# Attention of a hybrid residual block: TensorE in the written order, and 128 columns in place of padded 256

## The chip, the cores and the metric

The kernel runs on one core of a Trainium2 chip. The metric is the device time of one execution in microseconds (us). The engines are TensorE (PE, with its weight loads shown apart as PEld), VectorE (DVE), ScalarE (ACT), GpSimd (POOL) and SyncE (SP), which issues most of the transfers. Matrix products are written to PSUM, which has eight banks of 128 partitions x 512 fp32.

## The reference

One layer over x of shape (1, 512, 1024), all in fp32:

```
xn = rmsnorm(x)
q, k, v, xr, gr, ga, gb = split(xn @ W_in)          # each 512 x 1024
ya = chunked_band_attention(q, k, v, rel_table) @ W_attn_out
yb = (rg_lru(conv(xr)) * gelu(gr)) @ W_rnn_out
h  = x + (sigmoid(ga) * ya + sigmoid(gb) * yb) @ W_o
h  = h + (silu(g) * up) @ W_ffn_out                 # g, up = split(rmsnorm(h) @ W_ffn_in)
out = rmsnorm(h)
```

The attention has 16 heads of width 64. A frame belongs to a chunk of 64 and reads its own chunk and the eight before it, so over 512 frames it reads all earlier chunks: the probabilities are block lower triangular. A learned bias on the clipped distance is added to the scores, and a softmax follows.

## The kernel before

Precision: each fp32 operand is split into a high and a low part of type float32r (`split`, L78: ACT copies the high part, DVE subtracts to get the low one), and a product is three matmuls, high x high, high x low and low x high (`mm3`, L72, lines 74 to 76). In the attention the scores and the weighing use two (lines 651, 652 and 690), because both parts of one operand are laid beside each other on the 128 partitions.

Stages: the two first projections with the recurrent branch; the product with W_rnn_out (`po_yb`, lines 722 to 727); the attention (lines 728 to 734), interleaved with the projections that it still needs; the product with W_attn_out (`po_ya`); W_o; and the feed-forward block. The attention works by pairs of heads. For each pair, `q_tile` and `k_tile` (L593, L604) project xn to a 128 x 512 tile of 24 matmuls with 512 columns and convert it: Q with two ACT and two DVE instructions, K with four ACT (L611, L613), two DVE and two POOL instructions, because every head wants its copy in both halves of the partitions. `v_tile` (L627) projects one block of 128 frames for four heads, 24 matmuls with 256 columns, and `gate` (L560) makes one tile of the gates.

A head h is worked in three steps. `scores(h)` (L638) takes the four blocks of 128 queries in turn. Block qb has (qb + 1) x 128 keys: two matmuls, then on DVE the bias and a minimum (L654), then on ACT the exponential (L655); after the four, DVE takes the reciprocal of the sums (L656) and POOL scales the four blocks (L658). `transposed(h)` (L661) turns the ten 128 x 128 blocks of probabilities on TensorE into three PSUM tiles, one for the first 128 keys (four blocks), one for the second (three), and one for the third and fourth (two and one), and splits them into `pp`. `weigh(h)` (L679) multiplies by V: two matmuls for each block of keys, with as many columns as it has queries, into one PSUM tile, which ACT and DVE add into `oacc` and, after the second head of a pair, split into `aT`.

Two of the products are wider than their content. The scores of the first query block have 128 keys and are computed for 256 (`wm = max(w, 256)`). The weighing with the last 128 keys has 128 queries and is done for 256, over a part of `pp` that POOL sets to zero (L664).

PSUM: the tag `mm` has four banks, `s` and `t` two each. In the attention the projections, the weighing, the third transposed tile and the scores of query block 2 use `mm`; the other score blocks use `s`; the first two transposed tiles use `t`.

Order: a scheduler orders each engine's instructions from dependencies, from the order in which they are written and from its own estimate of the times, and sets the semaphores. It may move an instruction of TensorE ahead of others that were written earlier. The written order of the attention loop is: transposes of head h, scores of head h + 1, some projections, weighing of head h, some projections. Which projections is settled by `fill`: it takes the steps (Q, K, V and gate tiles, in the order in which the heads need them) from one list, with a weight of 1 for a Q, K or gate tile and 0.5 for a V tile, up to 1.25 + 1.5 h before the weighing and 2.0 + 1.5 h behind it.

Weights arrive through SP in pieces of 128 x 1024 (`load`, L137) and are split by ACT and DVE into four buffers (`prefetch`, L217), one group ahead of the projection that asks for them.

Of the kernel before, what the change touches and what calls it, by code (L numbers as in the profile page):

```python
# [8 lines left out]
F32 = mybir.dt.float32  # L9
# [5 lines left out]
P = 128  # L15
D = 1024
S = 512
KT = D // P
NT = S // P
HEADS = 16  # L20
# [16 lines left out]
def block_kernel(ctx: ExitStack, tc: tile.TileContext, x, norm_mix_g, w_in, b_merge, rel_table,  # L37
# [3 lines left out]
    pe, dve, act, pool, sp = nc.tensor, nc.vector, nc.scalar, nc.gpsimd, nc.sync  # L41
# [21 lines left out]
    ps = ctx.enter_context(tc.tile_pool(name="ps", bufs=2, space=PSUM))  # L63
    dr = ctx.enter_context(tc.tile_pool(name="dr", bufs=1, space=bass.MemoryType.DRAM))

    def f(ap):
        return ap.bitcast(F32)

    def mm_tile(name, tag="mm"):
        return ps.tile([P, S], F32, tag=tag, bufs=4 if tag == "mm" else 2, name=name)  # L70
# [7 lines left out]
    def split(hi, lo, src):  # L78

        act.activation(hi, src, AF.Copy)  # L80
        dve.tensor_sub(lo, src, f(hi))  # L81
# [161 lines left out]
    def weights(name, ahead=1):  # L243
        prefetch(index[name] + 1 + ahead)
        return made[index[name]]
# [116 lines left out]
    def features(pl, tag, name):  # L362

        t = pl.tile([P, KT, 2, S], F32R, tag=tag, name=name)
        return t, [t[:, k] for k in range(KT)]
# [13 lines left out]
    _, xnT = features(xnp, "xn", "xnT")  # L379
# [165 lines left out]
    def tile_of(name, c, tag="mm", ahead=1):  # L545

        whl = weights(name, ahead)
        if (name, c) in first:
            po = first[name, c]
            project(po, whl, c, xnT, 256, S)  # L550
        else:
            po = mm_tile(f"po_{name}_{c}", tag)
            project(po, whl, c, xnT)
        return po
# [5 lines left out]
    def gate(w, j):  # L560
        po = tile_of(f"g{'ab'[w]}{j - j % 2}", j % 2)
        act.activation((ta, zB)[w][j], po[:], AF.Tanh, bias=hb[:, 16 + 8 * w + j:17 + 8 * w + j], scale=0.5)
# [27 lines left out]
    def qk_pool(pr):  # L590
        return aw if pr % 2 else qkp

    def q_tile(pr):  # L593
        po = mm_tile(f"po_q{pr}")
        project(po, weights(f"qk{pr}"), 0, xnT)
        q = qk_pool(pr).tile([P, 2, S], F32R, tag="qk", bufs=3, name=f"q{pr}")
        for e in range(2):
            own, other = halves(e)
            src = backwards(po[own, :])
            act.activation(blocks(q[own, e]), src, AF.Copy, scale=0.125)  # L600
            dve.scalar_tensor_tensor(blocks(q[other, e]), src, 0.125, blocks(f(q[own, e])), ALU.mult, ALU.subtract)
        qk[pr] = [q]

    def k_tile(pr):  # L604
        po = mm_tile(f"po_k{pr}")
        project(po, weights(f"qk{pr}"), 1, xnT)
        kh = qk_pool(pr).tile([P, 2, S], F32R, tag="qk", bufs=3, name=f"kh{pr}")
        kl = qk_pool(pr).tile([P, 2, S], F32R, tag="qk", bufs=3, name=f"kl{pr}")
        for e in range(2):
            own, other = halves(e)  # L610
            act.activation(kh[own, e], po[own, :], AF.Copy)  # L611
            dve.tensor_sub(kl[own, e], po[own, :], f(kh[own, e]))
            act.activation(kh[other, e], po[own, :], AF.Copy)  # L613
            pool.tensor_copy(kl[other, e], kl[own, e])
        qk[pr] += [kh, kl]
# [11 lines left out]
    def v_tile(gr, t):  # L627
        wv = weights(f"v{gr}")
        po = mm_tile(f"po_v{gr}_{t}", "mm" if gr else "t")
        for k in range(KT):  # L630
            mm3(po[:, 0:256], xnT[k][:, 0, t * P:(t + 1) * P], xnT[k][:, 1, t * P:(t + 1) * P],
                wv(0, k, whole), wv(1, k, whole), k == 0, k == KT - 1)
        v = aw.tile([P, 2, 4, HD], F32R, tag="v", bufs=8, name=f"v{gr}_{t}")
        split(v[:, :, 0::3], v[:, :, 1:3], po[:, 0:256].rearrange("p (a b d) -> p a b d", a=2, b=2))
        vs.setdefault(gr, []).append(v)


    def scores(h):  # L638
        pr, e = divmod(h, 2)
        q, kh, kl = qk[pr]  # L640
        bias = bias_tile(h)
        lsum = cp.tile([P, NT], F32, tag="lsum", bufs=2, name=f"l{h}")
        nmax = cp.tile([P, NT], F32, tag="nmax", bufs=2, name=f"m{h}")
        rl = cp.tile([P, NT], F32, tag="rl", bufs=2, name=f"rl{h}")
        prob = [aw2.tile([P, (qb + 1) * P], F32, tag=f"p{qb}", name=f"p{h}_{qb}") for qb in range(NT)]
        for qb in range(NT):
            w = (qb + 1) * P
            wm = max(w, 256)
            sc = mm_tile(f"s{h}_{qb}") if qb == 2 else ps.tile([P, S], F32, tag="s", bufs=2, name=f"s{h}_{qb}")
            qs = q[:, e, qb * P:(qb + 1) * P]  # L650
            pe.matmul(sc[:, 0:wm], qs, kh[:, e, 0:wm], start=True, stop=False)
            pe.matmul(sc[:, 0:wm], qs, kl[:, e, 0:wm], start=False, stop=True)  # L652

            dve.tensor_tensor_reduce(prob[qb][:], sc[:, 0:w], bias[:, S - w:S], -1.0, 3e38, ALU.add, ALU.min, nmax[:, qb:qb + 1])  # L654
            act.activation(prob[qb][:], prob[qb][:], AF.Exp, bias=nmax[:, qb:qb + 1], scale=-1.0, accum_out=lsum[:, qb:qb + 1])  # L655
        dve.reciprocal(rl[:], lsum[:])  # L656
        for qb in range(NT):
            pool.tensor_scalar(prob[qb][:], prob[qb][:], rl[:, qb:qb + 1], 1.0, ALU.mult, ALU.mult)  # L658
        return prob

    def transposed(h, prob):  # L661

        pp = [aw2.tile([P, 2, S], F32R, tag="pt", bufs=4, name=f"pp{h}_{i}") for i in range(3)]
        pool.memset(f(pp[2][:, :, 256:384]), 0.0)  # L664
        for i, kbs in enumerate(((0,), (1,), (2, 3))):
            pt = mm_tile(f"pT{h}_{i}") if i == 2 else ps.tile([P, S], F32, tag="t", bufs=2, name=f"pT{h}_{i}")
            for kb in kbs:
                for qb in range(kb, NT):
                    at = qb - min(kb, 2) if kb < 3 else 2
                    pe.transpose(pt[:, at * P:(at + 1) * P], prob[qb][:, kb * P:(kb + 1) * P], ident[:])  # L670
            for at, lo, n in (((0, 0, 512),), ((0, 0, 384),), ((0, 0, 256), (384, 256, 128)))[i]:
                split(pp[i][:, 0, at:at + n], pp[i][:, 1, at:at + n], pt[:, lo:lo + n])
        return pp

    aT = []
# [3 lines left out]
    def weigh(h, pp):  # L679
        pr, e = divmod(h, 2)  # L680
        own, other = halves(e)
        if e == 0:
            oacc.append(tg_.tile([P, S], F32, tag="tg", name=f"oacc{pr}"))
        acc = oacc[pr]
        po = mm_tile(f"o{h}")
        for kb in range(NT):
            i, lo, n = ((0, 0, 512), (1, 0, 384), (2, 0, 256), (2, 256, 256))[kb]
            st = vs[pr // 2][kb][:, pr % 2, 2 * e:2 * e + 2].rearrange("p a d -> p (a d)")
            for part in range(2):
                pe.matmul(po[:, S - n:S], st, pp[i][:, part, lo:lo + n], start=kb == 0 and part == 0, stop=kb == NT - 1 and part == 1)  # L690
        act.activation(acc[own, :], po[other, :], AF.Copy)
        dve.tensor_add(acc[own, :], po[own, :], acc[own, :])
        if e == 1:
            if pr % 2 == 0:
                aT_pairs.append(rnp.tile([P, 2, 2, S], F32R, tag="big", bufs=4, name=f"aT{pr}"))
            o = aT_pairs[-1][:, pr % 2]
            split(blocks(o[:, 0]), blocks(o[:, 1]), backwards(acc[:]))
            aT.append(o)


    steps = []
    for pr in range(1, HEADS // 2):
        steps.append((1.0, lambda pr=pr: q_tile(pr)))
        steps.append((1.0, lambda pr=pr: k_tile(pr)))
        if pr in (2, 4, 6):
            for t in range(NT):
                steps.append((0.5, lambda pr=pr, t=t: v_tile(pr // 2, t)))
    for j in range(4, KT):
        steps.append((1.0, lambda j=j: gate(0, j)))
    spent = 0.0  # L710

    def fill(upto):
        nonlocal spent
        while steps and spent < upto:
            w, what = steps.pop(0)
            what()
            spent += w

    for t in range(NT):
        v_tile(0, t)  # L720
# [1 line left out]
    for j in range(KT):  # L722
        if j == 6:
            prob = scores(0)
        po = mm_tile(f"po_yb{j}")
        project(po, weights(f"yb{j - j % 2}"), j % 2, rnn)
        dve.scalar_tensor_tensor(zB[j], zB[j], 1.0, po[:], ALU.add, ALU.mult)
    for h in range(HEADS):
        pp = transposed(h, prob)
        if h + 1 < HEADS:  # L730
            prob = scores(h + 1)
        fill(1.25 + 1.5 * h)
        weigh(h, pp)
        fill(2.0 + 1.5 * h)
    aw2_stack.close()
    wo_stack, wop = opened("wo", 4)
    extra["wo1"] = wop
# [3 lines left out]
    _, mT = features(xnp, "xn", "mT")  # L741
# [113 lines left out]
    sc_stack, sc = opened("sc", 2)  # L855
# [83 lines left out]
    ks = list(range(0, FT, 4))  # L939
# [17 lines left out]
    for i, ((t, at), po) in enumerate(zip(pieces, pos)):  # L957
        for k0, wf in zip(ks[late:], wfs):
            out_tile(t, po, k0, wf, at)
        n = 1 + i // 4  # L960
# [30 lines left out]
```

## Time and profile before

| What | Value |
|---|---|
| Median of 3 runs | 888.18 us (887.58 to 888.22) |
| The profiled execution | 887.22 us, with a span of 885.4 us |
| TensorE busy | 871.9 us, 98% of the span |
| DVE, ACT, POOL busy | 548.4, 472.7 and 112.1 us |
| Matmuls | 5220 |
| Granted clock of TensorE | 1.00 |
| The attention loop | from about 248 to 441 us of the span |

A row of the time line gives the start in us, the length, the engine, the line, the operation, the tile written, the tiles read, the shapes and a count where equal instructions were merged; in brackets stands the idle time before it and what ended it. A matmul's row is longer than the time until the next one can start, because matmuls overlap in the array; spacing is read from start to start. In a window's row the busy times of PE, PEld, DVE, ACT and POOL follow the length, each with its number of instructions.

### The profile page before, as it was taken

To read this page: it belongs to the slowest core of one execution; us is meant where nothing else is said; L and a number is where in the kernel's file an instruction comes from. 1 tells how busy PE (TensorE), PEld (TensorE's weight loads), DVE (VectorE), ACT (ScalarE), POOL (GpSimd) and SP (SyncE) were. 2 spreads that over 40 slices of the span, in tenths; PEclk is the share of its full clock that TensorE was granted. 3 is DMA by queue.
4 is the path that set the end of the run, shared out by engine and by line. 5 is a ranking of instruction groups with operands and counts; after the bars stand their busy time and mean duration, and the time that the engine had idled before them with its cause. 6 is when DMAs were issued, how large, how long until landed. Compare 5 with 4: busy or idle time off the path is not lost.

```text
span 885.4 us, 13311 instructions
## 1 busy us (share of the span) xinstructions
PE 871.9 (98%) x5220; PEld 776.5 (88%) x5220; DVE 548.4 (62%) x872; ACT 472.7 (53%) x839; POOL 112.1 (13%) x157
## 2 busy tenths in 40 slices
PE   7999999999999999999999999999999999999997
PEld 5988888888888889898888889999999999888886
DVE  5776556563456675665447556888878887553203
ACT  7566646652256676676533466656555555723203
POOL 4013112220022222322100000000000001300100
PEclk9999999999999999999999999999999999999999
DMA  7223233433333233232223720524333332353002
GB/s 266 89 79 106 85 95 95 121 95 95 97 95 95 72 91 89 72 97 83 59 79 126 261 72 25 163 77 126 113 95 95 101 127 84 121 180 124 28 1 96
DMA packets 86080, 90.11 MB, mean 102 GB/s; under 512 B 5376, under 2 KB 74608, under 8 KB 86016
## 3 DMA queue, kind: packets, MB, share of 16 engines
q1 hardware_dynamic: 84640, 85.78, 31.5%
q10 hardware_dynamic: 1376, 3.47, 1.0%
q8 instruction: 41, 0.67, 0.3%
q14 instruction: 23, 0.19, 0.1%
HBM read 87.10 MB, written 2.14 MB: 101 GB/s over the span
## 4 chain that ended last, share of the span: by engine, by line
PE 96%; DVE 1%; SPq 1%; DMA 1%; ACT 1%; issue 1%; POOL 0%; ACTq 0%
PE po_out L74 5%; PE po_out L75 5%; PE po_out L76 5%; PE p_fg L74 2%; PE o L690 2%; PE p_fg L76 2%; PE p_fu L76 2%; PE p_fu L75 2%; PE p_fg L75 2%; PE p_fu L74 2%; PE pT L670 2%; PE po_v L75 2%; PE po_v L76 2%; PE po_v L74 2%; PE po_q L74 2%; PE po_q L75 2%
## 5 line engine op out<-in xcount | busy, mean ns | idle before, releaser
L75 PE MATMUL po_out<-whl_fo,act_hi 128*128 128x512 f32 (+1 forms) x198 | 72.5, 366 | 0.0
L74 PE MATMUL po_out<-whl_fo,act_hi 128*128 128x512 f32 (+1 forms) x198 | 72.3, 366 | 0.0
L76 PE MATMUL po_out<-whl_fo,act_lo 128*128 128x512 f32 (+1 forms) x198 | 71.7, 365 | 0.0
L81 DVE TENSOR_TENSOR whl_fo<-raw_fo,whl_fo 128x1024 fp32r<-128x1024 f32 x22 | 27.8, 1273 | 44.3 <-ACT whl_fo L80 43.9
L658 POOL TENSOR_SCALAR p<-p,rl 128x128 f32<-128x128 f32 (+1 forms) x64 | 36.1, 587 | 142.0 <-DVE rl L656 142.0
L875 POOL TENSOR_TENSOR act_lo<-act,act_hi 128x1024 fp32r<-128x1024 f32 x4 | 10.9, 2719 | 322.9 <-ACT act_hi L874 320.8
L80 ACT ACTIVATE whl_fo<-raw_fo 128x1024 fp32r<-128x1024 f32 x22 | 23.0, 1059 | 48.9 <-PE po_out L76 33.9
L654 DVE CUSTOM_DVE_ANT_0 p<-s,bias 128x384 f32<-128x384 f32 (+2 forms) x64 | 29.6, 485 | 21.5 <-PE s L652 20.9
L76 PEld LDWEIGHTS po_out<-whl_fo,act_lo 128*128 128x128 f32 x198 | 37.3, 189 | 6.0
L74 PEld LDWEIGHTS po_out<-whl_fo,act_hi 128*128 128x128 f32 x198 | 37.4, 189 | 6.0
L75 PEld LDWEIGHTS po_out<-whl_fo,act_hi 128*128 128x128 f32 x198 | 37.4, 189 | 5.9
L655 ACT ACTIVATE p<-p,m 128x384 f32<-128x384 f32 (+2 forms) x64 | 35.7, 561 | 12.6 <-DVE m L654 12.2
L76 PE MATMUL po_v<-whl_v,xnT 128*128 128x256 f32 x128 | 36.2, 283 | 0.0
L75 PE MATMUL po_v<-whl_v,xnT 128*128 128x256 f32 x128 | 36.2, 282 | 0.0
L74 PE MATMUL po_v<-whl_v,xnT 128*128 128x256 f32 x128 | 36.1, 282 | 0.0
L81 DVE TENSOR_TENSOR pp<-pT,pp 128x512 fp32r<-128x512 f32 (+1 forms) x64 | 29.3, 485 | 5.3 <-ACT pp L80 5.0
L75 PE MATMUL po_xr<-xnT,whl_xr 128*128 128x512 f32 (+1 forms) x80 | 27.9, 354 | 0.6 <-DVE xnT L358 0.6
L81 DVE TENSOR_TENSOR whl_fg_s<-s_fg,whl_fg_s 128x1024 fp32r<-128x1024 f32 x20 | 25.6, 1295 | 3.7 <-ACT whl_fg_s L80 3.7
L74 PE MATMUL po_gr<-xnT,whl_gr 128*128 128x512 f32 (+1 forms) x80 | 27.8, 349 | 0.1
L76 PE MATMUL po_gr<-xnT,whl_gr 128*128 128x512 f32 (+1 forms) x80 | 27.5, 348 | 0.3 <-DVE whl_gr L81 0.3
L75 PE MATMUL po_gr<-xnT,whl_gr 128*128 128x512 f32 (+1 forms) x80 | 27.6, 347 | 0.0
L74 PE MATMUL po_xr<-xnT,whl_xr 128*128 128x512 f32 (+1 forms) x80 | 26.6, 351 | 0.8 <-ACT xnT L357 0.8
(348 smaller groups left out, 3044.9 us busy)
## 6 DMA issues: line engine op xcount, KB each, us to landing
raw_fg<-in_w_ffn_in_dram SPq DMA_DIRECT2D x24, 512.0 KB, 4.5
raw_fu<-in_w_ffn_in_dram SPq DMA_DIRECT2D x22, 512.0 KB, 3.8
raw_fo<-in_w_ffn_out_dram SPq DMA_DIRECT2D x22, 512.0 KB, 4.2
raw_qk<-in_w_in_dram SPq DMA_DIRECT2D x32, 256.0 KB, 3.1
raw_xr<-in_w_in_dram SPq DMA_DIRECT2D x8, 512.0 KB, 4.6
raw_gr<-in_w_in_dram SPq DMA_DIRECT2D x8, 512.0 KB, 3.4
raw_ga<-in_w_in_dram SPq DMA_DIRECT2D x8, 512.0 KB, 3.9
raw_gb<-in_w_in_dram SPq DMA_DIRECT2D x8, 512.0 KB, 3.6
```

The source lines that it names most:

```text
L74: pe.matmul(o, sh, mh, start=start, stop=False, skip_group_check=parts)
L75: pe.matmul(o, sh, ml, start=False, stop=False, skip_group_check=parts)
L76: pe.matmul(o, sl, mh, start=False, stop=stop, skip_group_check=parts)
L80: act.activation(hi, src, AF.Copy)
L81: dve.tensor_sub(lo, src, f(hi))
L654: dve.tensor_tensor_reduce(prob[qb][:], sc[:, 0:w], bias[:, S - w:S], -1.0, 3e38, ALU.add, ALU.min, nmax[:, qb:qb + 1])
L655: act.activation(prob[qb][:], prob[qb][:], AF.Exp, bias=nmax[:, qb:qb + 1], scale=-1.0, accum_out=lsum[:, qb:qb + 1])
L658: pool.tensor_scalar(prob[qb][:], prob[qb][:], rl[:, qb:qb + 1], 1.0, ALU.mult, ALU.mult)
L670: pe.transpose(pt[:, at * P:(at + 1) * P], prob[qb][:, kb * P:(kb + 1) * P], ident[:])
L690: pe.matmul(po[:, S - n:S], st, pp[i][:, part, lo:lo + n], start=kb == 0 and part == 0, stop=kb == NT - 1 and part == 1)
L875: (pool if i in (0, 1, 2, 4) else dve).tensor_sub(lo[:], o[:], f(hi[:]))
```

## The change

Three things change, all within the attention.

1. The loop over the heads is put into a block in which the instructions of TensorE keep the order in which they are written; the other engines are ordered as before. `fill` and its list of steps go. In their place `laid(h)` gives each head a list of tiles that come before the weighing and one of tiles that come behind it: for heads 4m to 4m + 3, with m from 0 to 2, the Q tile of pair 2m + 2 before (for m = 0, Q and K of pair 1 before and Q of pair 2 behind); K of pair 2m + 2 before and the first V tile of the next group behind; the second and third V tile before and the fourth behind; Q of pair 2m + 3 before and its K behind. Heads 12 to 15 have one tile of the gates each, before.
2. The scores of the first query block, and the weighing with the last 128 keys, are computed with 128 columns. The zeroing on POOL goes, and the third transposed tile is split by one pair of instructions over 384 columns in place of two over 256 and 128.
3. The scores of query block 3 take their bank from `mm` in place of `s`.

```diff
@@ scores
-            wm = max(w, 256)
-            sc = mm_tile(f"s{h}_{qb}") if qb == 2 else ps.tile([P, S], F32, tag="s", bufs=2, name=f"s{h}_{qb}")
+            sc = mm_tile(f"s{h}_{qb}") if qb >= 2 else ps.tile([P, S], F32, tag="s", bufs=2, name=f"s{h}_{qb}")
             qs = q[:, e, qb * P:(qb + 1) * P]
-            pe.matmul(sc[:, 0:wm], qs, kh[:, e, 0:wm], start=True, stop=False)
-            pe.matmul(sc[:, 0:wm], qs, kl[:, e, 0:wm], start=False, stop=True)
+            pe.matmul(sc[:, 0:w], qs, kh[:, e, 0:w], start=True, stop=False)
+            pe.matmul(sc[:, 0:w], qs, kl[:, e, 0:w], start=False, stop=True)
@@ transposed
-        pool.memset(f(pp[2][:, :, 256:384]), 0.0)
...
-            for at, lo, n in (((0, 0, 512),), ((0, 0, 384),), ((0, 0, 256), (384, 256, 128)))[i]:
-                split(pp[i][:, 0, at:at + n], pp[i][:, 1, at:at + n], pt[:, lo:lo + n])
+            n = (512, 384, 384)[i]
+            split(pp[i][:, 0, 0:n], pp[i][:, 1, 0:n], pt[:, 0:n])
@@ weigh
-            i, lo, n = ((0, 0, 512), (1, 0, 384), (2, 0, 256), (2, 256, 256))[kb]
+            i, lo, n = ((0, 0, 512), (1, 0, 384), (2, 0, 256), (2, 256, 128))[kb]
@@ the order
-    steps = []
...
-    def fill(upto):
...
+    def laid(h):
+        m, at = divmod(h, 4)
+        qs, ks, va = (lambda pr: lambda: q_tile(pr)), (lambda pr: lambda: k_tile(pr)), (lambda t: lambda: v_tile(m + 1, t))
+        if h >= 12:
+            return [lambda: gate(0, h - 8)], []
+        first_, second = 2 * m + 2, 2 * m + 3
+        return {0: (([qs(1), ks(1)] if m == 0 else []) + ([] if m == 0 else [qs(first_)]), [qs(first_)] if m == 0 else []),
+                1: ([ks(first_)], [va(0)]),
+                2: ([va(1), va(2)], [va(3)]),
+                3: ([qs(second)], [ks(second)])}[at]
@@ the loop
-    for h in range(HEADS):
-        pp = transposed(h, prob)
-        if h + 1 < HEADS:
-            prob = scores(h + 1)
-        fill(1.25 + 1.5 * h)
-        weigh(h, pp)
-        fill(2.0 + 1.5 * h)
+    with tc.manual_schedule(engines={mybir.EngineType.PE}):
+        for h in range(HEADS):
+            pp = transposed(h, prob)
+            if h + 1 < HEADS:
+                prob = scores(h + 1)
+            before, after = laid(h)
+            for what in before:
+                what()
+            weigh(h, pp)
+            for what in after:
+                what()
```

More of the change, by code (lines that the diff above doesn't have):

```diff
@@ L698, in weigh @@
             aT.append(o)
-    steps = []
[L702 to L710, printed above, removed]
-    def fill(upto):
[L713 to L717, printed above, removed]
+    def laid(h):
[8 more added lines that the diff above has]
+                3: ([qs(second)], [ks(second)])}[at]
     for t in range(NT):
```

## The prediction

> **What bounds the kernel now.** I read the page's first part, then the busy time by window over the attention, then what TensorE waited for, then its instructions in order of time at each wait. The busy share and the two windows come first (columns of a window: its length, then busy us of PE, PEld, DVE, ACT and POOL, then the granted clock).
>
> ```profile
> span 885.4 us, 13311 instructions
> PE 871.9 (98%) x5220; PEld 776.5 (88%) x5220; DVE 548.4 (62%) x872; ACT 472.7 (53%) x839; POOL 112.1 (13%) x157
> ...
> 252.00:430.00 178.00, 176.01 (x1041) 155.95 (x1041) 115.51 (x267) 118.24 (x267) 46.78 (x97) 1.00 0.30 85
> 430.00:442.00 12.00, 11.79 (x59) 9.60 (x58) 4.40 (x10) 5.12 (x11) 2.06 (x4) 1.00 0.13 39
> ...
> PE s L651 <- ACT kh L613: 2.0, 4, 0.5
> ```
>
> TensorE is the bound: 98% busy over the kernel, 176.01 of 178 us in the attention, at full clock. DVE and ACT are each busy for two thirds of the attention. So an order of TensorE can win only what TensorE loses to waits, and the one wait the profile names there is on the conversion of K (L613): four times, 2.0 us together. A busy matmul row is longer than the time it takes from the next one, so I price waits from start to start:
>
> ```profile
> 311.26 1.25 PE L670 MATMUL pT<-ident,p 128*128 128x128 f32 x10
> 313.01 0.68 PE L651 MATMUL s<-kh,q 128*128 128x256 f32 x3 [0.49 <-ACT kh L613]
> ...
> 332.62 0.86 PE L690 MATMUL o<-pp,v 128*128 128x384 f32 x5
> 333.47 0.38 PE L651 MATMUL s<-kh,q 128*128 128x256 f32 x1
> 333.69 0.28 PE L652 MATMUL s<-kl,q 128*128 128x256 f32 x1
> ...
> 433.94 1.47 PE L670 MATMUL pT<-ident,p 128*128 128x128 f32 x6
> 435.17 0.47 PE L74 MATMUL po_ga<-xnT,whl_ga 128*128 128x512 f32 x1
> ```
>
> ```profile
> 302.15 0.39 PE L75 MATMUL po_q<-xnT,whl_qk 128*128 128x512 f32 x1
> 302.38 0.39 PE L76 MATMUL po_q<-xnT,whl_qk 128*128 128x512 f32 x1
> ...
> 249.16 0.34 PE L651 MATMUL s<-kh,q 128*128 128x384 f32 x1
> 249.34 0.33 PE L652 MATMUL s<-kl,q 128*128 128x384 f32 x1
> 249.51 0.39 PE L74 MATMUL po_q<-xnT,whl_qk 128*128 128x512 f32 x1
> ...
> 295.62 0.28 PE L75 MATMUL po_v<-whl_v,xnT 128*128 128x256 f32 x1
> 295.74 0.28 PE L76 MATMUL po_v<-whl_v,xnT 128*128 128x256 f32 x1
> ...
> 295.62 0.19 PEld L76 LDWEIGHTS po_v<-whl_v,xnT 128*128 128x128 f32 x1
> ```
>
> Undisturbed spacings: 0.227 us at 512 columns, 0.17 at 384, 0.12 at 256 and, for the ten transposes of 1.25 us (the last one 0.27), (1.25-0.27)/9 = 0.11. A projection of 24 products is 24 x 0.227 = 5.45 us, a tile of V 24 x 0.12 = 2.9, a head's transposes 1.1. Its eight products of scores, and likewise its eight of the weighing, are 2 x (0.227 + 0.17 + 0.12 + 0.12) = 1.27.
>
> **What the change takes away.** (a) The K wait. The last transpose starts at 311.26 + 9 x 0.11 = 312.25, the first score at 313.01: 0.76 where 0.11 is due, 0.65 lost, four times: 2.6 us. In the lists `k_tile` of a pair stands one or two heads before the scores that read it (K of pair 3 behind head 3, its scores in the round of head 5, with 6.7 us of weighing and projection and two heads' transposes between), so this wait goes. What is late next is priced below. (b) The six transposes at 433.94 take 435.17 - 433.94 = 1.23 where 6 x 0.11 is due: 0.6 lost to the normalization of the probabilities. (c) At 333 the last weighing product starts at 332.62 + 0.86 - 0.28 = 333.20 and the two scores at 333.47 and 333.69: 0.49 for 0.24, 0.25 lost; the same stands in two more heads, 0.75. Together **3.95 us**, the most the new order can return.
>
> **The columns.** Four products of each head, 64 in all, go from 256 to 128 columns. At 256 they are spaced 0.12, not half of the 0.227 of 512: the weight load of L76 begins at 295.62, when the product before it begins, and its own product begins 0.12 later. Weights are always 128x128, so a product of 128 columns should still wait 0.12 for the next weights; the transposes, with 128 columns and weights of the same size, stand at 0.11. I take 0.115: 64 x 0.005 = **0.3 us gained**. Bounds: half of 0.12 would gain 64 x 0.06 = 3.8; a narrow product that takes the time of four passes over 128 columns (the 512-column row, 0.227) would lose 64 x 0.107 = 6.8.
>
> The Trainium skill, TensorE: Matmul & The Clock Gate, Back-to-back issue gap, gives about 81 ns for each pair of weight load and 128-column matmul in a stream, with which the 64 would gain an estimated 2.5 us and the sum would come to 885.2; it belongs to the third rival below. The transposes' 110 ns speak against it here.
>
> **What the change adds.** TensorE now takes each head as written: ten transposes, eight scores of the next head, the list `before`, eight products of the weighing, the list `after`. Three things can be late.
>
> ```profile
> 310.19 0.60 ACT L611 ACTIVATE kh<-po_k 64x512 fp32r<-64x512 f32 x1 [1.60 <-PE po_k L76]
> 310.68 1.05 ACT L80 ACTIVATE whl_v<-raw_v 128x1024 fp32r<-128x1024 f32 x1
> 311.75 0.59 ACT L691 ACTIVATE oacc<-o 64x512 f32<-64x512 f32 x1
> 312.37 0.59 ACT L613 ACTIVATE kh<-po_k 64x512 fp32r<-64x512 f32 x1
> ...
> 270.39 0.39 PE L652 MATMUL s<-kl,q 128*128 128x512 f32 x1
> 272.81 2.07 POOL L658 TENSOR_SCALAR p<-p,rl 128x128 f32<-128x128 f32 x4 [6.66 <-DVE rl L656]
> ...
> 304.30 0.39 PE L652 MATMUL s<-kl,q 128*128 128x512 f32 x1
> 307.95 3.04 POOL L658 TENSOR_SCALAR p<-p,rl 128x128 f32<-128x128 f32 x4 [10.19 <-DVE rl L656]
> ...
> 307.47 0.29 DVE L81 TENSOR_TENSOR pp<-pT,pp 128x128 fp32r<-128x128 f32 x1
> ```
>
> (1) PSUM banks. Tag "mm" has four. The scores of the fourth query block move into it from "s", so every head now takes pT2, s2, s3, its projections and o from that ring. Behind K (heads 3, 7, 11) come ten transposes and eight scores, 1.1 + 1.27 = 2.4 us, and then a projection that needs a bank while K, pT2, s2 and s3 hold all four. K's own release takes four ACT instructions at 0.61 each (311.75 to 312.37), 2.4, with 0.16 until the last product is out (0.39 - 0.23) and about 0.3 for the hops and the weight load (0.12): 2.95. Wait: about 0.6, three times, 1.8. Before the second tile of V in heads 2, 6 and 10 all four banks are held likewise; the tile before it needs only one ACT and one DVE pass, but ACT owes K's four (2.4), two weight conversions of 1.05, and about 1.2 for o and its split, 5.7 us of work in the 4.2 us of weighing and V tile: 1.5 behind, then about 1.2 for its own: 2.7 against 2.4. Wait 0.3, three times, 0.9. The gates of heads 12 to 15 I give 0.3 together.
>
> (2) The probabilities. From a head's last score to its last POOL scaling before: 274.88 - 270.39 = 4.5 us, and 310.99 - 304.30 = 6.7 where weight conversions ran beside it. The shortest cover in the lists is one projection and the weighing, 5.45 + 1.27 = 6.7, plus 0.33 until the fourth transpose, which reads the last block (heads 4, 8 and 12 to 14). It holds, barely: I give 0.1 in each of five, 0.5. The other heads have 9.6 us and more.
>
> (3) The split before the weighing: transposes begin at 302.61, the last split ends at 307.76, 5.2 us; the cover is transposes, scores and at least 5.45 of projection, 7.8. Hidden.
>
> Sum of (1) and (2): 1.8 + 0.9 + 0.3 + 0.5 = **3.5 us added**. Ends: none of it (every bank free in time), and half a 1.05 conversion more at each of the twelve places, 3.5 + 6.3 = 9.8.
>
> **The rest.** The zeroing on POOL goes, and the two splits of the third transposed tile become one. POOL is busy for 46.78 of 178 us and the instructions lie off the chain: nothing, while (2) and (3) have slack; where a head is at its end it shortens it by under 0.3. Weight loads and bias loads keep their order on SP; the weights of the next projection group are converted when the group before last lets its buffers go, 9 us or more ahead. With TensorE waiting below 1 us at a time, the clock, 1.00 in both windows, should stay.
>
> **The sum.** -3.95 - 0.3 + 3.5 = -0.75. The profiled execution took 887.22 us (span 885.4), the median is 888.18, 0.96 above it; the difference is applied to the median: **887.4 us**. What a measurement of this kernel tells from no change is 0.2%, 1.8 us, so I forecast no change that counts.
>
> **Rivals.**
> *Slower: the bank ring.* ACT and DVE stand further behind at the seven bank places and the five short covers than I take. It decides from (0.75 + 1.8)/12 = 0.21 us more at each. With half a conversion more: 888.18 - 0.75 + 6.3 = 893.7. For it: TensorE can no longer take a product of a projection while a score waits, which in the time before it does (249.51, 270.39). Against: the waits that showed there were four, of 0.5.
> *Slower: narrow products cost more.* At 0.227 each, +6.8; about 2 of that is cover for the waits of (1) and (2): 888.18 - 0.45 + 4.8 = 892.5. No run here has a 128-column product that is not a transpose, so nothing excludes it.
> The Trainium skill, FP8 and Floating Point Precision, TensorE Precision Notes, says that true FP32 takes four passes through the array and reduced precision does not; no row here shows whether width bears on that.
> *Faster: narrow products at half.* 0.06 each, -3.8, of which about 1 comes back as waits: 888.18 - 0.45 - 2.8 = 884.9. Against: the 0.11 of the transposes.
> *Faster: the new waits stay out.* The conversions that hold the banks are taken in time: 888.18 - 3.95 - 0.3 = 883.9. For it: ACT and DVE have a third of their time free; against: the work bunches behind K.
> That the order would not be kept is covered by the forecast: the columns alone would give 887.9.
>
> **How the numbers follow.** Forecast 0.28 (with added waits of 2.5 to 5 us its own range is 886.4 to 888.9); bank ring 0.20; costlier narrow products 0.18; half-price narrow products 0.12; no new waits 0.22. Faster: 0.12 + 0.22 = 0.34; same 0.28; slower 0.20 + 0.18 = 0.38. The range reaches to the rivals' times on both sides, 883.6 to 893.7.
>
> **What would show it.** K wait: no L651 row that waits for L613. Order: the scores of a head in one unbroken run after its transposes. Columns: start-to-start of the 128-column rows of L651 and L690, 0.11 to 0.12, against 0.06 or 0.23. Banks: waits in front of `po_q`, `po_v` and `po_ga` of heads 4, 8, 12 and 2, 6, 10, of 0.3 to 0.6, released by ACT or DVE on the oldest tile; if they exceed 1 us, the ring is the cause and I am wrong upward. Probabilities: waits of L670 on POOL L658 below 0.3 in heads 5, 9 and 13 to 15.

## The result and the profile after

The changed kernel takes 889.6 us (median of 20 runs, 888.85 to 890.73), the kernel before 887.34 us beside it (median of 20 runs, 887.13 to 888.49). The ratio is 1.0023, with a 95% interval from 1.0016 to 1.0029: slower by some 2.3 us. The three runs that the prediction started from had a median of 888.18, 0.84 above this one. The profiled execution took 888.87 us against 887.22, 1.65 more.

From the page of the changed kernel, its row of busy time; then the attention by window (length, busy time of PE, PEld, DVE, ACT and POOL, granted clock); then what TensorE waited for in the attention (total, times, longest, in us):

```profile
PE 870.7 (98%) x5220; PEld 775.2 (87%) x5220; DVE 551.2 (62%) x856; ACT 470.8 (53%) x823; POOL 105.3 (12%) x141
```
```profile
252.00:430.00 178.00, 172.60 (x1031) 152.72 (x1030) 113.44 (x246) 115.34 (x250) 41.94 (x83) 1.00 0.29 84
```
```profile
PE po_q L74 <- DVE m L653: 2.7, 2, 1.3
PE po_ga L74 <- DVE m L653: 1.3, 1, 1.3
PE po_k L74 <- DVE m L653: 1.2, 1, 1.2
```

The wait of the scores for K is gone from the list. In its place a projection waits four times, 1.2 to 1.3 us each, for the reduction of a score block on DVE (L653 here is L654 of the kernel before). TensorE is busy for 172.60 of the 178 us where it was 176.01, at the same full clock. One of the four places, in TensorE's order:

```profile
307.63 0.40 PE L76 MATMUL po_k<-xnT,whl_qk 128*128 128x512 f32 x1
307.87 1.25 PE L668 MATMUL pT<-ident,p 128*128 128x128 f32 x10
308.88 0.31 PE L650 MATMUL s<-kh,q 128*128 128x128 f32 x1
...
309.42 0.34 PE L650 MATMUL s<-kh,q 128*128 128x384 f32 x1
...
310.00 0.40 PE L651 MATMUL s<-kl,q 128*128 128x512 f32 x1
311.74 0.50 PE L74 MATMUL po_q<-xnT,whl_qk 128*128 128x512 f32 x1 [1.34 <-DVE m L653]
312.08 0.39 PE L75 MATMUL po_q<-xnT,whl_qk 128*128 128x512 f32 x1
```

K of pair 3 ends, the ten transposes of head 4 and the eight scores of head 5 follow without a gap, and then the Q of pair 4 starts 1.74 us after the last score where 0.227 is due: 1.51 lost, and 0.11 more on its second product (0.34 for 0.227). The rows of DVE and ACT over the same time tell which bank it waited for:

```profile
308.69 0.68 DVE L612 TENSOR_TENSOR kl<-po_k,kh 64x512 fp32r<-64x512 f32 x1 [1.04 <-ACT kh L611]
...
309.65 0.42 DVE L653 CUSTOM_DVE_ANT_0 p<-s,bias 128x256 f32<-128x256 f32 x1
...
309.99 1.22 DVE L81 TENSOR_TENSOR whl_v<-raw_v,whl_v 128x1024 fp32r<-128x1024 f32 x1
311.13 0.55 DVE L653 CUSTOM_DVE_ANT_0 p<-s,bias 128x384 f32<-128x384 f32 x1
...
312.21 0.68 DVE L653 CUSTOM_DVE_ANT_0 p<-s,bias 128x512 f32<-128x512 f32 x1
...
312.81 1.02 DVE L81 TENSOR_TENSOR pp<-pT,pp 128x384 fp32r<-128x384 f32 x2
313.86 0.69 DVE L612 TENSOR_TENSOR kl<-po_k,kh 64x512 fp32r<-64x512 f32 x1
```
```profile
314.59 0.60 ACT L613 ACTIVATE kh<-po_k 64x512 fp32r<-64x512 f32 x1 [0.20 <-DVE kl L612]
```

Four tiles hold the banks of `mm`. K is read until 314.59 + 0.60 = 315.19, the third transposed tile until 312.81 + 1.02, score block 3 until 312.21 + 0.68, all later than the start at 311.74. Only score block 2 is done, at 311.13 + 0.55 = 311.68. So Q gets the bank of score block 2, and what holds it is DVE's order: the first subtraction of K, two reductions and a weight conversion of 1.22 us stand before that reduction. (This is read from the times, as the profile does not name banks; the experiments below test it.)

At head 1 the same happens behind a Q, without a weight conversion. K of pair 2 starts at 271.32, 0.07 after the reduction of block 2 has ended, while Q's bank is read until after 272.37. Here two splits of transposed tiles stand between:

```profile
268.37 0.68 DVE L601 SCALAR_TENSOR_TENSOR q<-po_q,q 64x512 fp32r<-64x512 f32 x1 [2.98 <-ACT q L600]
269.08 0.69 DVE L81 TENSOR_TENSOR pp<-pT,pp 128x512 fp32r<-128x512 f32 x1
...
269.89 0.55 DVE L81 TENSOR_TENSOR pp<-pT,pp 128x384 fp32r<-128x384 f32 x1
...
270.70 0.55 DVE L653 CUSTOM_DVE_ANT_0 p<-s,bias 128x384 f32<-128x384 f32 x1
...
271.32 0.50 PE L74 MATMUL po_k<-xnT,whl_qk 128*128 128x512 f32 x1 [1.25 <-DVE m L653]
...
272.37 0.69 DVE L601 SCALAR_TENSOR_TENSOR q<-po_q,q 64x512 fp32r<-64x512 f32 x1
```

Start to start, the places at 271, 312, 361 and 411 us lose 1.42 and three times 1.51, the gate of head 14 loses 0.28, and the second product behind each of the five about 0.11: 6.8 us. Everything else by which the spacings between 230 and 450 us exceed the undisturbed ones (the prediction's 0.227, 0.17 and 0.12, and 0.109 where it rounds to 0.11) fell from 5.4 us to 0.8. (The stretch goes to 450 because the last weighing of the kernel before starts at 448.5, behind the 441 of its table.) That leaves 6.8 - 4.6 = 2.2 more waiting, less 64 x 0.011 = 0.7 by the narrower products: 1.5, against 1.65 between the two profiled executions.

### The profile page after: what moved, and what is told of

The parts are those of the page before. It is cut to its first block, busy times and chain, and to the rows that moved or that the text cites. A ratio compares the mean times of both kernels' runs of the same rounds, so it can differ in the third digit from the quotient of the medians.

```text
span 887.1 us, 13322 instructions
## 1 busy us (share of the span) xinstructions
PE 870.7 (98%) x5220; PEld 775.2 (87%) x5220; DVE 551.2 (62%) x856; ACT 470.8 (53%) x823; POOL 105.3 (12%) x141
## 4 chain that ended last, share of the span: by engine, by line
PE 95%; DVE 2%; ACT 1%; DMA 1%; issue 0%; ACTq 0%; DVEq 0%
PE po_out L75 5%; PE po_out L76 5%; PE po_out L74 5%; PE p_fg L74 2%; PE o L688 2%; PE p_fg L76 2%; PE p_fu L76 2%; PE p_fu L75 2%; PE p_fg L75 2%; PE p_fu L74 2%; PE po_v L74 2%; PE po_ga L74 2%; PE po_v L76 2%; PE po_v L75 2%; PE po_q L74 2%; PE po_k L74 2%
## 5 line engine op out<-in xcount | busy, mean ns | idle before, releaser
L654 ACT ACTIVATE p<-p,m 128x128 f32<-128x128 f32 (+1 forms) x64 | 35.8, 562 | 11.1 <-DVE m L653 10.7
L653 DVE CUSTOM_DVE_ANT_0 p<-s,bias 128x128 f32<-128x128 f32 (+1 forms) x64 | 29.7, 484 | 0.7 <-issue 0.5
L81 DVE TENSOR_TENSOR whl_qk<-raw_qk,whl_qk 128x1024 fp32r<-128x1024 f32 x16 | 20.9, 1308 | 14.3 <-ACT whl_qk L80 14.3
L75 PE MATMUL po_xr<-xnT,whl_xr 128*128 128x512 f32 (+1 forms) x80 | 27.9, 354 | 0.6 <-DVE xnT L358 0.5
L74 PE MATMUL po_q<-xnT,whl_qk 128*128 128x512 f32 x64 | 25.3, 395 | 2.7 <-DVE m L653 2.7
L81 DVE TENSOR_TENSOR pp<-pT,pp 128x384 fp32r<-128x384 f32 (+1 forms) x48 | 27.9, 596 | 0.0
L74 PE MATMUL po_gr<-xnT,whl_gr 128*128 128x512 f32 (+1 forms) x80 | 27.8, 349 | 0.1
L76 PE MATMUL po_gr<-xnT,whl_gr 128*128 128x512 f32 (+1 forms) x80 | 27.5, 348 | 0.3 <-DVE whl_gr L81 0.3
```

Source lines behind the costliest of these rows:

```text
L74: pe.matmul(o, sh, mh, start=start, stop=False, skip_group_check=parts)
L75: pe.matmul(o, sh, ml, start=False, stop=False, skip_group_check=parts)
L76: pe.matmul(o, sl, mh, start=False, stop=stop, skip_group_check=parts)
```

## The experiments

"Before" is the kernel before, run beside each of these kernels on the same chip; a ratio is the time of the kernel against it, with a 95% interval. The medians of before lie between 887.3 and 887.5.

### The parts by themselves

The written order with the old widths: the changed kernel with `wm = max(w, 256)`, the zeroing, two splits and 256 columns back.

```diff
-            pe.matmul(sc[:, 0:w], qs, kh[:, e, 0:w], start=True, stop=False)
+            pe.matmul(sc[:, 0:wm], qs, kh[:, e, 0:wm], start=True, stop=False)
...
-            i, lo, n = ((0, 0, 512), (1, 0, 384), (2, 0, 256), (2, 256, 128))[kb]
+            i, lo, n = ((0, 0, 512), (1, 0, 384), (2, 0, 256), (2, 256, 256))[kb]
```

> The changed kernel with 256 columns, the zeroing and the two splits put back: the written order and the bank of the fourth score block alone. Theory A (columns gain 2.2, and the order loses what the bank waits cost): about 2.2 us above the changed kernel, 891.8 us, 4.5 above before. If the columns were worth only 0.3: about 889.9.

Measured: 890.21 us, ratio 1.0031 (1.0019 to 1.0044). The waits are there at the same places, start to start 1.96, three times 1.79, and 0.45, where the changed kernel has 1.65, three times 1.74, and 0.51. So the order brings the loss (with the bank of the fourth score block, which a run below takes back), and beside it the columns are worth 0.6 us by the medians, which the intervals of the two kernels do not separate from nothing; 0.4 of it lies in the waits.

The 128 columns without the order: the kernel before with `wm = w`, no zeroing, one split, and 128 in the weighing; `fill` and the scheduler's order stay.

> The kernel before with its scheduler and fill, and only the columns changed: 128 for the first scores and the last keys, no zeroing on POOL, the third transposed tile split in one. Theory A (in the changed kernel the second of two 128-column products starts 0.06 us after the first and the next product 0.11 after that, 0.17 for a pair where 256 columns take 0.24): 32 pairs x 0.07 = 2.2 us gained, about 885.1 us against 887.3 before. Rival, the prediction's own price (0.3 us for all 64): 887.0, no difference. Rival, narrow products cost more: above 888.

Measured: 897.07 us, ratio 1.0111 (1.0097 to 1.0124), 9.6 us slower. Of the three expectations only the last lies on that side, with narrow products as the cause; the next two runs speak against that cause. These two kernels take the halves apart: the scores at 128 columns alone, and the weighing at 128 with one split and no zeroing alone.

```diff
-            wm = max(w, 256)
+            wm = w
```

> The kernel before with the first query block's scores at 128 columns and nothing else; the weighing stays at 256 with its zeroing and two splits. Theory (the 128 columns are worth what the weight loads leave, 0.015 us a head for two score products, and the 9.6 us of the kernel with both edits came from the scheduler's other order): TensorE's order stays the one before, 887.2, between 886.8 and 887.7; waits of L651 on L613 stay near 2.0 us. Rival (128 columns in the scores cost time themselves, through the banks of s that come free at another moment): above 889.

```diff
-        pool.memset(f(pp[2][:, :, 256:384]), 0.0)
...
+            n = (512, 384, 384)[i]
+            split(pp[i][:, 0, 0:n], pp[i][:, 1, 0:n], pt[:, 0:n])
...
-            i, lo, n = ((0, 0, 512), (1, 0, 384), (2, 0, 256), (2, 256, 256))[kb]
+            i, lo, n = ((0, 0, 512), (1, 0, 384), (2, 0, 256), (2, 256, 128))[kb]
```

> The kernel before with the weighing of the last 128 keys at 128 columns, without zeroing and with one split, and nothing else. Theory: it is this half that makes the scheduler lay TensorE's work out anew in the attention; so most of the 9.6 us appear here, 893 to 898, with waits of L651 on L613 above 4 us and stretches in which 512-column products stand 0.43 apart. Rival (it takes both halves): 886.5 to 888, with waits as before.

Measured: the scores alone 886.89 us, ratio 0.9993 (0.9984 to 1.0002), with TensorE's instructions in exactly the order of before and the same row for the wait on K (2.0, 4, 0.5); the weighing alone 896.9 us, ratio 1.011 (1.0095 to 1.0126), with another order of TensorE from the second head on. What TensorE waits for in the latter:

```profile
PE s L651 <- ACT kh L613: 5.8, 4, 2.4
PE pT L669 <- POOL p L658: 1.9, 2, 1.2
```

With this half (the narrow weighing, one split, no zeroing) the scheduler, which goes by its own estimate of the times, lays the attention out anew, and two of the four waits on K grow to 2.4 us. Each is followed by one on POOL, and by products at half speed. Rows of TensorE at the first place, and the same place by window:

```profile
313.29 0.70 PE L651 MATMUL s<-kh,q 128*128 128x256 f32 x2 [2.35 <-ACT kh L613]
...
315.60 1.14 PE L669 MATMUL pT<-ident,p 128*128 128x128 f32 x3 [1.19 <-POOL p L658]
...
319.10 0.63 PE L75 MATMUL po_q<-xnT,whl_qk 128*128 128x512 f32 x1
319.53 0.63 PE L76 MATMUL po_q<-xnT,whl_qk 128*128 128x512 f32 x1
```
```profile
310.01:313.42 3.41, 1.06 (x8) 0.91 (x7) 2.77 (x4) 3.34 (x7) 0.60 (x1) 1.00 0.87 196
313.42:320.25 6.83, 5.64 (x18) 4.48 (x19) 2.66 (x10) 3.42 (x10) 2.81 (x6) 0.50 0.33 96
320.25:324.00 3.75, 3.75 (x20) 3.10 (x20) 0.35 (x2) 0.81 (x2) 2.20 (x5) 1.00 0.23 70
```

At 319.10 the 512-column products stand 0.43 apart, not 0.227; the granted clock is 0.50 from 313.42, just behind the wait on K, to 320.25, and 1.00 on both sides. The place at 313 and its like at 414 lose 6.7 and 5.5 us where the kernel before loses 0.9 at each, 10.4 more; the rest of the attention loses about 1 us less, which leaves 9.4 for the 9.5 between the medians. What the columns-only kernel, with the same two waits of 2.4 us, shows is thus a price of the scheduler's order, not of narrow products. Which of the three edits tips that order was not followed further.

### Which bank, and what holds it

If the ring of `mm` is the cause, a tile that takes a bank elsewhere does not wait. K of pair 2, Q of pairs 4 and 6 and the gates of heads 12 and 14 take theirs from `s`:

```diff
-    def q_tile(pr):
-        po = mm_tile(f"po_q{pr}")
+    def q_tile(pr, tag="mm"):
+        po = mm_tile(f"po_q{pr}", tag)
...
-        qs, ks, va = (lambda pr: lambda: q_tile(pr)), (lambda pr: lambda: k_tile(pr)), (lambda t: lambda: v_tile(m + 1, t))
+        qs, ks, va = (lambda pr: lambda: q_tile(pr, "s" if at == 0 and m else "mm")), (lambda pr: lambda: k_tile(pr, "s" if h == 1 else "mm")), (lambda t: lambda: v_tile(m + 1, t))
```

> The changed kernel with one edit: the tile that follows the scores in heads 1, 4, 8, 12 and 14 (K of pair 2, Q of pairs 4 and 6, two gates) is written to a bank of tag s in place of mm; the order of TensorE stays as it is. Theory A (TensorE waits there only for a bank of the ring, 1.4 + 3 x 1.5 + 0.3 = 6.2 us, and the two banks of s are free 1.6 us earlier): those five waits vanish, 883 to 884 us. Rival (the waits come from DVE and ACT being behind as such, and the bank is only where it shows): TensorE waits as long at the next place that needs them, 888 to 890 us.

Measured: 886.11 us, ratio 0.9987 (0.9978 to 0.9995), between the two expectations. The waits before `po_q` are gone; now the scores of the next head wait for Q to give its bank back, in two heads, and of the five places the gate of head 14 still waits. What TensorE waits for in the attention:

```profile
PE s L650 <- DVE q L601: 1.4, 2, 0.7
PE po_ga L74 <- DVE m L653: 0.4, 1, 0.4
PE s L650 <- ACT kh L613: 0.2, 1, 0.2
```

By the spacings 4.6 us are lost in the attention where the changed kernel loses 7.6. So the bank is what the projections wait for, and a part of the waiting moves to the other ring. The other direction, the changed kernel with the fourth score block back in `s`, which leaves `mm` one tile less per head:

```diff
-            sc = mm_tile(f"s{h}_{qb}") if qb >= 2 else ps.tile([P, S], F32, tag="s", bufs=2, name=f"s{h}_{qb}")
+            sc = mm_tile(f"s{h}_{qb}") if qb == 2 else ps.tile([P, S], F32, tag="s", bufs=2, name=f"s{h}_{qb}")
```

> The changed kernel with the fourth score block back in tag s: the ring mm has one tile less to hold. Then its first product needs the reduction of block 0, which in the changed kernel ended at 309.72 where the product began at 309.77, and later where DVE is behind: a wait of 0 to 1 us in each of 15 heads, the four waits of 1.5 us gone or smaller. Theory A (both rings bind, the ring s in every head): 890 to 896 us. Rival (only the ring mm binds): 884.

Measured: 891.79 us, ratio 1.0049 (1.0035 to 1.0062).

```profile
PE s L650 <- DVE m L653: 5.3, 9, 1.0
```

The waits before the projections are gone, but in nine heads the fourth block waits for the reduction of an earlier one in `s`. Under the written order the move of that block to `mm` pays; it is not the part that costs.

Next, what stands in DVE's way. Weight conversions put behind the last reduction and exponential of the head:

```diff
+                elif behind[0] is not None:
+                    with tc.issue_after(behind[0].ins), tc.issue_after(behind[1].ins):
+                        split(hl[:, 0], hl[:, 1], raw[:])
```

> The changed kernel with one edit: in the attention the conversions of weights (128x1024, 1.05 us on ACT and 1.22 on DVE) are issued on each of the two engines behind the last reduction and the last exponential of the scores written before them; banks and TensorE's order stay. Theory B (the bank that the projection waits for is held by the reduction of score block 2, which stands behind one conversion of 1.22 us on DVE): the four waits of 1.5 us shrink to about 0.3 each, 884 to 885 us. Rival (the bank is held by the slow release of K, which has nothing to do with the conversion): no change, 889.5. Conversions that come too late for their projection would show as waits on whl_ tiles.

Measured: 888.91 us, ratio 1.0017 (1.0009 to 1.0026); start to start the waits stay at 1.64 and three times 1.52. The subtractions of the splits have moved into the place of the conversion:

```profile
310.43 0.67 DVE L81 TENSOR_TENSOR pp<-pT,pp 128x512 fp32r<-128x512 f32 x1
...
311.24 0.54 DVE L81 TENSOR_TENSOR pp<-pT,pp 128x384 fp32r<-128x384 f32 x1
...
312.05 0.54 DVE L658 CUSTOM_DVE_ANT_0 p<-s,bias 128x384 f32<-128x384 f32 x1
```

So the conversion alone is not the cause. With the subtractions put behind the reduction of block 2 as well:

```diff
+            act.activation(pp[i][:, 0, 0:n], pt[:, 0:n], AF.Copy)
+            owed.append((pp[i][:, 1, 0:n], pt[:, 0:n], f(pp[i][:, 0, 0:n])))
...
+            with tc.issue_after(third[0].ins):
+                for args in owed:
+                    dve.tensor_sub(*args)
```

> The changed kernel with DVE's order alone changed: the subtractions that split the transposed tiles are issued behind the reduction of score block 2, and the conversions of weights behind the scores (as in the run with the conversions behind). TensorE's order and the banks stay. Theory B2 (the projection waits for the bank of score block 2, and DVE reaches its reduction only after K's or Q's first subtraction, two split subtractions and, in the changed kernel, one conversion): the reduction ends at 0.9 us behind the scores in place of 1.7, the four waits go from 1.5 to about 0.5 us, 885 to 886 us. Rival (it is K's bank that matters): no change from 888.9.

Measured: 886.86 us, ratio 0.9993 (0.9984 to 1.0002). The reduction comes directly behind the two before it, and the projection starts 0.61 after the last score (309.77 to 310.38) where it was 1.74:

```profile
309.77 0.40 PE L657 MATMUL s<-kl,q 128*128 128x512 f32 x1
310.38 0.50 PE L74 MATMUL po_q<-xnT,whl_qk 128*128 128x512 f32 x1 [0.21 <-DVE m L661]
```
```profile
309.76 0.55 DVE L661 CUSTOM_DVE_ANT_0 p<-s,bias 128x384 f32<-128x384 f32 x1
...
310.24 1.61 DVE L737 TENSOR_TENSOR pp<-pT,pp 128x512 fp32r<-128x512 f32 x3
```
```profile
PE pT L677 <- POOL p L665: 1.4, 4, 0.3
```

That is the direct test: TensorE's order is untouched, DVE's is changed, and 1.1 us go at each of the four places. Against the run before it, from which it differs in the subtractions alone, 0.9 us go (1.52 to 0.61). About half comes back as waits of the transposes for the scaled probabilities, 2.5 us start to start.

### Lists without a Q or K directly ahead of the transposes

If a tile that holds its bank long is the trouble only when ten transposes and eight scores follow it, then other lists suffice. The second K of each group goes to the front of the next list `before`; the Q of pair 2 goes ahead of the weighing of head 0.

```diff
-            return [lambda: gate(0, h - 8)], []
+            return ([ks(7)] if h == 12 else []) + [lambda: gate(0, h - 8)], []
...
-        return {0: (([qs(1), ks(1)] if m == 0 else []) + ([] if m == 0 else [qs(first_)]), [qs(first_)] if m == 0 else []),
+        return {0: (([qs(1), ks(1)] if m == 0 else [ks(2 * m + 1)]) + [qs(first_)], []),
...
-                3: ([qs(second)], [ks(second)])}[at]
+                3: ([qs(second)], [])}[at]
```

> The changed kernel with other lists: K of the second pair stands no longer behind the weighing of heads 3, 7 and 11 but first in the list before the weighing of heads 4, 8 and 12, and Q of pair 2 goes from behind the weighing of head 0 to before it; so only V tiles and the weighing itself stand directly ahead of the transposes and scores. Theory A (the waits of 1.4 to 1.5 us come from a Q or K tile that still holds its bank and DVE when the scores take the other three): the four waits go, the round of heads 3, 7, 11 gets the short cover of 6.7 us for its probabilities and may wait up to 0.5 us each; 883 to 885 us. Rival (any projection behind the scores waits for the reduction of block 2): waits of about 1 us at more places, 888 or above.

Measured: 883.51 us (882.29 to 884.01), ratio 0.9951 (0.9938 to 0.9963): faster than both kernels. No wait of TensorE is named in the attention; its window:

```profile
252.00:430.00 178.00, 177.90 (x1065) 158.59 (x1064) 118.43 (x256) 118.48 (x259) 47.83 (x87) 1.00 0.30 87
```

One wait is left start to start, 0.27 before the gate of head 14. The same lists with 256 columns:

> The lists of the run before with 256 columns, the zeroing and the two splits. It gives the worth of the columns where the bank waits are out of the way. Weight loads bind (0.11 us from load to load): 0.5 to 1 us above the run with 128 columns, as between the changed kernel and its 256-column version (0.6). If the narrow pair of 0.17 us counted in full: 2.2 us above.

Measured: 883.1 us (882.71 to 884.4), ratio 0.9952 (0.9939 to 0.9964). By the medians the columns gain nothing here: the kernel with 256 is 0.4 us lower, and the runs of each kernel spread over 1.7 us. In the two traces the stretch from the first transpose to the product behind the last weighing is 189.74 us with 128 columns and 190.58 with 256.

## Why the prediction was wrong

**What bounds the kernel.** Right: TensorE's waits in the attention decide, and DVE and ACT, busy for the same 62% and 53%, matter only through what they hold.

**What the change takes away.** Right in kind: no score waits for K, the transposes of the last heads run without a gap, and the 0.25 at the scores went. 4.6 us went, by the spacings, where the sum had 3.95 as the most that could.

**The columns.** Right that the weight loads bind, for three of the four narrow products of a head. In the changed kernel the loads of the scores start 0.11 apart:

```profile
308.85 0.19 PEld L650 LDWEIGHTS s<-kh,q 128*128 128x128 f32 x1
308.96 0.19 PEld L651 LDWEIGHTS s<-kl,q 128*128 128x128 f32 x1
309.07 0.19 PEld L650 LDWEIGHTS s<-kh,q 128*128 128x128 f32 x1
```

The two narrow products of the scores stand 0.14 and 0.11 apart, so the rival by which they cost 0.227 falls. The rival of half the price is true for one product in four: of the two that end the weighing, the second starts 0.06 behind the first (318.37 and 318.43 below), and the next transpose 0.11 behind the second, at 318.54. The prediction had 0.11 to 0.12 for all of them. The two products, and the second alone:

```profile
318.37 0.33 PE L688 MATMUL o<-pp,v 128*128 128x128 f32 x2
...
318.43 0.27 PE L688 MATMUL o<-pp,v 128*128 128x128 f32 x1
```

The Trainium skill, TensorE: Matmul & The Clock Gate, Back-to-back issue gap, states a pace of 81 ns for such pairs in a stream. The trace does not agree: the three loads above give 110.

The term was too small. The first four products of the scores take 309.42 - 308.88 = 0.54, and 0.56 in the written order with 256 columns. The eight of the weighing take 1.21 against 1.28; first the rows of the changed kernel, then those of the written order with 256 columns:

```profile
317.33 1.37 PE L688 MATMUL o<-pp,v 128*128 128x512 f32 x8
318.54 1.28 PE L668 MATMUL pT<-ident,p 128*128 128x128 f32 x10
```
```profile
317.95 1.44 PE L690 MATMUL o<-pp,v 128*128 128x512 f32 x8
319.23 1.25 PE L670 MATMUL pT<-ident,p 128*128 128x128 f32 x10
```

That is 16 x 0.09 = 1.4 us at these products, against 0.3 in the sum. Over the whole stretch of the two traces without waits 0.84 is left, and the medians, 0.6 one way and 0.4 the other, do not settle it.

**PSUM banks.** This is the step that failed. The place was right, behind K in heads 3, 7 and 11, and so was the sign that I named for being wrong upward, waits above 1 us. Three things in the working were not.

- "K's own release takes four ACT instructions" put the release 2.95 us after K's last product (2.4, 0.16 and 0.3, as they stand there, make 2.9). K is read until 315.19, 7.2 us after the end of its last product (307.63 + 0.40 = 308.03): the second subtraction stands on DVE behind reductions and splits, and the last copy on ACT comes after it. The bank that comes free first is score block 2's. Its release is a sum over DVE's order, which I did not make for these places: 0.6 predicted, 1.62 measured (1.51 + 0.11), three times, so 4.9 for 1.8.
- The Q tile behind the weighing of head 0 is followed by transposes and scores just as K is. I left that place out: 1.5 us.
- The second V tile, for which I gave 0.9, never waited, and neither did the transposes for the probabilities (0.5). The gate of head 14 lost 0.4 where 0.3 stood for all gates.

Together 6.8 us for 3.5. The upper end, half a conversion more at each of twelve places, held for the total (6.8 below 9.8) but not for its reason: the places are five, each of the three behind K took 1.0 us more than predicted where half a conversion is 0.5, and a conversion is only one of the things that can stand ahead.

**The sum.** -0.75 against +1.65 in the profiled executions: 3.3 too little waiting, less about 0.65 and 0.4 for what was removed and the columns. That 889.6 lies only 2.2 above the forecast of 887.4 flatters it: the sum was taken off a median of three runs, and from the 887.34 measured beside the changed kernel it gives 886.6, so the change was missed by 3.0 us. No change that counts was forecast, and the kernel became slower. The rival of the bank ring came nearest: a bank is what TensorE waits for, but at five places and not twelve, and at a smaller price than the 893.7 it was given.

**The clock.** Right in its outcome: the window still has 1.00, though the waits are idle stretches of 1.3 and not below 1 us.

**That the order would not be kept.** "The columns alone would give 887.9" was wrong by 9 us: I costed them with the order of before, while a small edit of sizes lets the scheduler choose another.

## What to carry to other kernels

When an engine is put in program order, list for each of its tiles which PSUM bank it needs and which instruction gives that bank back, and sum the work that stands ahead of that instruction in its own engine's queue; the duration of the reading instructions alone says little. Where such a wait shows, change first what stands directly ahead of the burst of short tiles (here: keep Q and K away from transposes and scores, -6 us against the changed kernel), before moving banks or work of DVE, which moved a part of the wait elsewhere. And test a small edit of sizes in a fixed order of instructions: under a scheduler its price can be that of another order (9.5 us here).

## What the runs showed of the hardware beyond that

The granted clock halves sooner than I had thought. In the weighing-only kernel it falls to 0.50 at 313.42 for 6.83 us and at 419.23 for 3.41 us. These lengths, and the 105.81 us between the two falls, are 2, 1 and 31 times 3.413 us, as if the clock were set anew at fixed steps of that length. In the steps ahead of the two falls TensorE was busy for 1.06 us (above) and for 1.50 of the 3.41:

```profile
415.82:419.23 3.41, 1.50 (x8) 1.11 (x9) 2.62 (x8) 2.60 (x7) 1.47 (x4) 1.00 0.50 174
419.23:422.65 3.42, 3.42 (x11) 2.83 (x11) 1.28 (x5) 2.00 (x6) 1.34 (x3) 0.50 0.05 16
```

So the longest wait alone does not decide: the same wait of 2.35 us ends 0.1 us ahead of the first fall and 2.3 us ahead of the second, which has another of 0.69 behind it. Single waits of 1.3 us in the changed kernel left the clock at 1.00. Nor does the busy time order all steps: in the columns-only kernel a step with 1.56 us (413.91 to 417.32) is followed by 1.00 and one with 1.78 (417.32 to 420.73) by 0.50. The second has transposes in it and the first has none; whether transposes count in full was not tested.

The Trainium skill, TensorE: Matmul & The Clock Gate, Part 1: The HAM clock gate (the "warmup" mystery), says that the clock drops after an idle window of about 3.4 us and comes back after about as much of sustained work, with a window that runs freely. The steps of 3.41 us and the way back fit that. The way down does not: the windows ahead of the two falls were busy for 1.06 and 1.50 us.
